# Low half of q in two zero-padded tiles per head pair, in a ten-phase transformer kernel

## The chip, the cores and the metric

The program runs on one core of a Trainium2 chip. The metric is the device time of one execution in microseconds (us), the median of several runs. Times in the profile are counted from the first instruction of the profiled execution. Engines: PE is TensorE (PEld its weight loads), DVE is VectorE, ACT ScalarE, POOL GpSimd, SP SyncE.

## The reference

One sequence of 512 tokens with 1024 features goes through two stacks. The first has two layers of half-step feed-forward, mixer, half-step feed-forward. Its mixers are a hybrid (8 heads of chunkwise retention and 8 heads of dilated attention) and a stick-breaking attention with 16 heads. The second stack has two layers of a mixer and a squared-ReLU feed-forward; its mixer has pooling and 8 heads of a sparse attention (NSA) in two groups, with a branch over compressed keys and two branches over all causal keys. All heads have 64 features. In every attention the scores are products of q and k over these 64 features:

```
s = einsum('...nqd,...nkd->...nqk', qb, kb) * dh ** -0.5      # dilated, NSA
z = einsum('bhqd,bhkd->bhqk', q_blk, kf) * dh ** -0.5         # stick-breaking
scores = einsum('bhnid,bhnjd->bhnij', qc, kc) * decay_in      # retention
```

Inputs, weights and the result are float32.

## The kernel before

**Precision.** Products keep near float32 accuracy by splitting each factor in a high half h (rounded to the type that TensorE multiplies) and a low half l, the rest. A projection's product is h h + h l + l h: three matmuls, lines 326 to 328 (`mm3`), or 734 to 737 where tokens are the output's rows (`tok_k`).

**Phases.** The order is F00, M0, F10, F01, M1, F11, N0, G0, N1, G1. F and G are feed-forwards, M0 the hybrid mixer, M1 the stick-breaking one, N0 and N1 the NSA mixers. The activations stay in SBUF, features on the partitions. Weights come in pieces of 512 KB over SyncE's queue and are split by ScalarE (L297) and by VectorE or, in N, GpSimd (L298).

**Order of the work in a mixer.** The class `Side` puts attention work between the matmuls of the projections. A unit, usually one head, goes through stages: A the scores, B the transposes or sums, C the product with v. A stage is put out once a planned time of products lies behind the stage before it (`N_LAT`, `M1_LAT`, `M0_LAT`); what a stage costs is a fixed number that its function returns. Within an engine the instructions run in the order in which they were put out, which a planner has fixed before.

**Two heads in one tile.** A pair tile has head A's 64 features in rows 0 to 63 and head B's in rows 64 to 127. `stacks` (L742 to 767) makes from it for q: Q with [qhA; qhA] and [qhB; qhB], and QL with [qlA; qlB]; for k: [khA; klA] and [klB; khB]. A score is then two matmuls. The first has all 128 rows and gives qh kh + qh kl at once; the second takes the low half of q with the high half of k of the same head and has the 64 rows of this head:

```
nc.tensor.matmul(ps[:, o:o + N], lhsT=Q[:, hd, qs], rhs=K[:, hd, :N], start=o == 0, stop=False, **kw)     # L861
nc.tensor.matmul(ps[:, o:o + N], lhsT=QL[sl, qs], rhs=K[sl, hd, :N], start=False, stop=True, **kw)        # L862
```

These two lines (`sm_scores`) serve dilated attention and NSA's two branches. For a head the queries go in four tiles of 128, and the causal part gives 512, 384, 128 and 256 columns (`PARTS`), eight matmuls in all. Retention has the same pair at L983 and L985 (`ret_A`), stick-breaking at L1140 and L1142 (`A` of `phase_M1`), there with two halves of the queries: blocks of 128 and 256 columns, then 256, 256, 128 and 256.

**NSA's compressed branch.** `Kc` holds the compressed keys of the two groups in six stationary tiles, the last two for QL (L1398 and L1399). `Vc` holds the compressed values [vh | vl] in rows of 32, so that the product with them (L1456) has 32 rows.

**Around it.** After the scores VectorE takes the row extremum (L866) and ScalarE the exponential (L868); VectorE and ScalarE scale (L877, L879); TensorE transposes (L892); ScalarE and VectorE split the result pTa, pTb (L336, L337); TensorE multiplies by v (L905), and `av_evac` (L908 to 914) adds the two row halves by way of a small tile avt. `n_consts` (L1241) loads the constants of an N phase over GpSimd's queue while the phase before runs: among them the mask cmask and the pooling weights pw. w1, the first layer for the compressed keys and values, is loaded at L1364 within N, and fl (L1498) is its input.

Of the kernel before, what the change touches and what calls it, by code (L numbers as in the profile page):

```python
# [64 lines left out]
# Mixers: PSUM banks (TAGS), the side work's share and latencies (R, LAT, DELAY, CAP; see Side), the ranges of the  # L65
# output projection (OUT), buffers
# [8 lines left out]
M0_AV = 2  # L75
# [18 lines left out]
# tiles of 512, 384, 256 and 128 columns: the part (bank) that holds each, and where  # L94
# [77 lines left out]
class Kern:  # L172
# [34 lines left out]
    # ---------------------------------------------------------------- weights  # L207
# [124 lines left out]
    def split(self, h, l, src, scale=None, leng=None):  # L332
        """h, l with h + l = scale * src; scale None, a power of two, or a column."""
# [8 lines left out]
    def rsqrt(self, out, v, n, tag):  # L342
        """out = v ** -0.5 on [P, n]."""
# [8 lines left out]
        if n <= 2:  # L352
            # a column at a time, with the factors as its scalars
# [51 lines left out]
    def token_sums(self, v, which, c0):  # L405
        """v[:, t] = the sums over the features of the squares, for the token tiles from token c0 on."""
# [20 lines left out]
    def bcast(self, col, tag="b"):  # L427
        """[P, n] token columns -> PSUM [P, n * 128], the same row in every partition."""
# [22 lines left out]
    def e_norm(self, hf, L, which, fn):  # L451
        """xg = x / rms(x) * norm * (1 + scale) + shift for a half of the tokens.

        With fn, x is first normed by final_norm; x itself follows in the next phase.
        A generator: it pauses after the sums and after the row of factors.
        """
# [8 lines left out]
        with self.tc.high_priority():  # L465
# [6 lines left out]
            if fn:  # L472
                # of v = mean(x^2) + eps and v2 = mean((x fnorm)^2): both factors are 1 / sqrt(v2 + eps v)
# [24 lines left out]
    def last_tiles(self, ds, rhs, ks, tag, etag, finish, ws=None):  # L498
        """Output tiles ds; before an explicit norm the last ones go by halves of the tokens."""
# [25 lines left out]
    def e_go(self, tag="b"):  # L525
        """The next step of the norms under way."""
# [12 lines left out]
    # ---------------------------------------------------------------- modulation  # L539
# [29 lines left out]
    # ---------------------------------------------------------------- feed-forward  # L569
# [155 lines left out]
    def tok_k(self, o, w, t, k, kc, width):  # L725
        """Token tile t, contraction tile k, which is kc of the weight piece w."""
# [5 lines left out]
        own = width > 256  # else two token tiles share a bank, which one start clears  # L732
# [6 lines left out]
    def v_evac(self, V, o, t, scale):  # L739
        """V[:, t, head] = [vh | vl] of o [P, heads * 64]."""  # L740
        self.split(V[:, t, :, 0:HD], V[:, t, :, HD:], o.rearrange("p (h e) -> p h e", e=HD), scale=scale)

    def stacks(self, pool, kind, src, scale=None, copies=True):
        """q: QA = [qhA; qhA], QB = [qhB; qhB], QL = [qlA; qlB]; k: KA = [khA; klA], KB = [klB; khB]."""
# [13 lines left out]
        if kind == "q":  # L758
            QL = pool.tile([P, S], F32R, name=self.name("ql"), tag="ql", bufs=self.nst[kind])
            low(QL[A], src, A, T[A, 0, :])  # L760
            low(QL[B], src, B, T[B, 1, :])
# [24 lines left out]
    def out_proj(self, gate, cuts):  # L786
        """x += gate * (o @ w_out), in passes over ranges of the contraction: all but the last run beside side work."""
# [13 lines left out]
        def pieces(n):  # L801
            """Weights of output tile after output tile."""
# [44 lines left out]

    def sm_scores(self, pool, Q, QL, K, sl, table, fac):
        """p = exp(s - max s) * fac / den per q tile; Q holds -q / 8 and table the negated addend to s."""
        nc = self.nc  # L850
        hd = 0 if sl.start == 0 else 1
# [3 lines left out]
        for i, qts in enumerate(PARTS):  # L855
            ps = self.ps.tile([P, S], F32, name=self.name("sc"), tag="b")
            for qt in qts:
# [4 lines left out]
                nc.tensor.matmul(ps[:, o:o + N], lhsT=QL[sl, qs], rhs=K[sl, hd, :N], start=False, stop=True, **kw)  # L862
# [35 lines left out]
    def av(self, ps, hl, V, first=True, last=True):  # L898
        """ps [P, S] += [vh | vl]^T (h + l); V(kt) the stationary [P, 128]."""
# [8 lines left out]
    def av_evac(self, pool, ps, o, hd):  # L908
        """o rows of the head = the two row halves of ps added."""
        nc = self.nc  # L910
        n = ps.shape[-1]
        t = pool.tile([HD, S], F32, name=self.name("avt"), tag="avt", bufs=self.navt)
        nc.scalar.activation(t[:, :n], ps[HD:], AF.Copy)
        nc.vector.tensor_tensor(o[HD * hd:HD * hd + HD], ps[:HD], t[:, :n], ALU.add)

    # ---------------------------------------------------------------- retention + dilated
    def rotary(self, pool, ps, cos, sin):
        """Both heads of a feature-major pair tile: ps * cos + swap(ps) * sin."""
# [11 lines left out]
    def phase_M0(self, ph, pool):  # L930
        nc, I = self.nc, self.I
        self.mixer_start()
        tabs = {}
# [34 lines left out]
        def ret_A(u):  # L968
# [4 lines left out]
            sl = slice(64 * hd, 64 * hd + 64)  # L973
            a = self.score_tiles(pool, F32, 0)
            hl = self.score_tiles(pool, F32R, 1)
            for i, parts in enumerate(PARTS):
                ps = self.ps.tile([P, S], F32, name=self.name("sc"), tag="b")
                w = 0
                for kt in (3 - j for j in parts):
# [5 lines left out]
                    nc.tensor.matmul(ps[:, o:o + N], lhsT=K[sl, hd, ks], rhs=QL[sl, kt * P:],  # L985
# [23 lines left out]
        def dil_A(u):  # L1009
            Q, QL, K, hd, h, V, o = u  # L1010
            u.append(self.sm_scores(pool, Q, QL, K, slice(64 * hd, 64 * hd + 64), lnc, None))
# [94 lines left out]
    # ---------------------------------------------------------------- stick-breaking  # L1106
    def phase_M1(self, ph, pool):
        nc, I = self.nc, self.I
        self.tc.keep_in_program_order(nc.scalar.preload_act_table_set("natural_log_exp_and_others"))
        smask = pool.tile([P, 2, 2 * P], F32, name="smask")  # L1110
        nc.gpsimd.dma_start(out=smask, in_=I["sbmask"])
        mraw = pool.tile([P, 2, P], F32, name="mraw")
# [4 lines left out]
        # blocks (key tile, first column, columns, first query) of a half of the queries  # L1117
        # the blocks on the diagonal are the columns from DG on
# [9 lines left out]

        def zap(zs, c, n):
            return zs[c // 512][:, c % 512:c % 512 + n]  # L1130

        def A(u):
            Q, QL, K, hd, h, V, o, half = u
            sl = slice(64 * hd, 64 * hd + 64)
            zs = [self.ps.tile([P, S], F32, name=self.name("z"), tag="z") for _ in BANKS[half]]
            for kt, c, n, q0 in BL[half]:
# [16 lines left out]
            self.pick(M1_MK[0]).tensor_tensor(e[:, DG[half]], e[:, DG[half]], smask[:, 0, :], ALU.mult)  # L1153
# [769 lines left out]
```

## Time and profile before

| | |
|---|---|
| median of 3 runs | 3391.49 us (3389.45 to 3393.52) |
| span of the profiled execution (the page lists this time of it alone) | 3388.5 us |
| median less that span | 3.0 us |
| busy: TensorE, VectorE, ScalarE, GpSimd | 3312.8, 1903.1, 1383.8, 769.6 us |
| matmuls | 15974 |
| HBM read, mean | 326.77 MB, 97 GB/s |

How to read it: a matmul's busy time includes its way through the array, and the next one starts before it ends, so busy times of TensorE overlap and say little about how fast it goes. The distance from the start of one matmul to the start of the next says it. PEclk is the granted clock of TensorE, 1.00 for 2.4 GHz and 0.50 for 1.2 GHz. Approximate places of the phases: M0 382 to 695, M1 1417 to 1736, N0 2090 to 2385, N1 2740 to 3040; the rest is feed-forwards.

### The profile page before, as it was taken

What the parts mean: (1) busy time and instruction counts of PE and PEld (TensorE: products, weight loads), DVE (VectorE), ACT (ScalarE), POOL (GpSimd) and SP (SyncE); (2) the same over time, 40 slices, a digit from 0 to 9 for tenths busy, and PEclk for the clock granted to TensorE, in tenths of its full rate; (3) what the DMA queues carried; (4) which work ended last, traced back from release to release, by engine and by line L of the source; (5) the groups of instructions that cost most, each with busy time, mean ns of one, the idle gap of its engine ahead of it and who ended that gap; (6) DMA issues with size and microseconds to landing.
All of it is one profiled execution on the core that took longest, in us unless ns stands there. A gap on an engine that the chain in (4) does not pass through costs nothing.

```text
span 3388.5 us, 41553 instructions
## 1 busy us (share of the span) xinstructions
PE 3312.8 (98%) x15974; PEld 2711.8 (80%) x15974; DVE 1903.1 (56%) x3115; ACT 1383.8 (41%) x2274; POOL 769.6 (23%) x712
## 2 busy tenths in 40 slices
PE   9999999999999999999999999889999989999999
PEld 7888888778888888888878888767888877688887
DVE  6633576866337634567853346776533377764332
ACT  4222466632223222477742224565322236633222
POOL 3111222121112110135531102442311143311111
PEclk9999999999999999999999999989999999899999
DMA  7623322165325623311123232201333221013222
GB/s 238 211 87 96 110 80 80 63 200 183 93 91 180 205 94 97 99 58 44 57 82 106 89 101 69 79 25 43 97 95 97 90 81 50 19 44 112 94 93 81
DMA packets 102645, 331.56 MB, mean 98 GB/s; under 512 B 11280, under 2 KB 19568, under 8 KB 102448
## 3 DMA queue, kind: packets, MB, share of 16 engines
q1 hardware_dynamic: 84944, 268.67, 24.9%
q0 software_dynamic: 17504, 60.24, 5.8%
q8 instruction: 126, 2.06, 0.3%
q14 instruction: 71, 0.58, 0.1%
HBM read 326.77 MB, written 2.10 MB: 97 GB/s over the span
## 4 chain that ended last, share of the span: by engine, by line
PE 91%; DVE 6%; ACT 1%; issue 1%; DMA 0%; POOL 0%; SPq 0%; ACTq 0%; DVEq 0%; POOLq 0%
PE po L326 10%; PE po L327 10%; PE po L328 10%; PE pu L327 5%; PE pu L328 5%; PE pu L326 5%; PE pg L327 5%; PE pg L326 5%; PE pg L328 5%; PE p L327 4%; PE p L328 4%; PE p L326 4%; PE pp L328 2%; PE pp L326 2%; PE pp L327 2%; PE av L905 2%
## 5 line engine op out<-in xcount | busy, mean ns | idle before, releaser
L297 ACT ACTIVATE wh<-wr 128x1024 fp32r<-128x1024 f32 (+2 forms) x516 | 535.7, 1039 | 1305.6 <-PE po L327 486.2
L298 DVE TENSOR_TENSOR wl<-wr,wh 128x1024 fp32r<-128x1024 f32 (+2 forms) x466 | 579.4, 1244 | 288.0 <-ACT wh L297 260.6
L327 PE MATMUL po<-hid,wh 128*128 128x512 f32 (+1 forms) x1276 | 489.0, 383 | 0.0
L328 PE MATMUL po<-hid,wl 128*128 128x512 f32 (+1 forms) x1276 | 488.3, 383 | 0.0
L326 PE MATMUL po<-hid,wh 128*128 128x512 f32 (+1 forms) x1276 | 487.6, 382 | 0.0
L337 POOL TENSOR_TENSOR hid<-fs,hid 128x512 fp32r<-128x512 f32 x88 | 143.2, 1627 | 876.0 <-ACT hid L336 875.9
L326 PEld LDWEIGHTS po<-hid,wh 128*128 128x128 f32 x1276 | 240.1, 188 | 49.8
L327 PEld LDWEIGHTS po<-hid,wh 128*128 128x128 f32 x1276 | 240.1, 188 | 48.9
L328 PEld LDWEIGHTS po<-hid,wl 128*128 128x128 f32 x1276 | 240.1, 188 | 48.4 <-DVE wl L298 0.5
L327 PE MATMUL p<-xg,wh 128*128 128x512 f32 (+1 forms) x576 | 215.0, 374 | 2.8 <-DVE xg L496 2.8
L328 PE MATMUL p<-xg,wl 128*128 128x512 f32 (+1 forms) x576 | 214.6, 373 | 0.1
L326 PE MATMUL p<-xg,wh 128*128 128x512 f32 (+1 forms) x576 | 213.4, 374 | 1.1 <-ACT fs L650 1.0
L337 POOL TENSOR_TENSOR hid<-g,hid 128x512 fp32r<-128x512 f32 x64 | 85.5, 1337 | 563.9 <-ACT hid L336 563.9
L591 DVE TENSOR_TENSOR fa<-pg,rB 128x512 f32<-128x512 f32 x88 | 60.3, 690 | 213.1 <-PE pg L328 201.1
L594 DVE TENSOR_TENSOR fs<-fs,pu 128x512 f32<-128x512 f32 x88 | 60.2, 686 | 212.8 <-PE pu L328 212.1
L559 DVE SCALAR_TENSOR_TENSOR wm<-wm,cact 128x1024 f32<-128x1024 f32 x96 | 125.6, 1311 | 89.4 <-DMA wm<-in_w_mod 85.9
L689 DVE SCALAR_TENSOR_TENSOR x<-po,modc,x 128x512 f32<-128x512 f32 (+1 forms) x68 | 48.8, 719 | 210.8 <-PE po L328 210.8
L326 PE MATMUL pu<-xg,wh 128*128 128x512 f32 x416 | 165.9, 399 | 0.0
L328 PE MATMUL pu<-xg,wl 128*128 128x512 f32 x416 | 165.6, 398 | 0.0
L327 PE MATMUL pu<-xg,wh 128*128 128x512 f32 x416 | 165.4, 398 | 0.0
L298 POOL TENSOR_TENSOR wl<-wr,wh 128x1024 fp32r<-128x1024 f32 (+2 forms) x50 | 117.6, 2354 | 208.0 <-ACT wh L297 151.4
L620 DVE TENSOR_TENSOR t<-po,rH 128x512 f32<-128x512 f32 (+1 forms) x100 | 66.8, 668 | 170.3 <-PE po L328 170.3
(406 smaller groups left out, 7745.6 us busy)
## 6 DMA issues: line engine op xcount, KB each, us to landing
wr<-in_ffn_w_in SPq DMA_DIRECT2D x174, 512.0 KB, 3.7
wr<-in_w_ff SPq DMA_DIRECT2D x128, 512.0 KB, 3.8
wm<-in_w_mod POOLq DMA_DIRECT2D x96, 512.0 KB, 4.6
wr<-in_ffn_w_out SPq DMA_DIRECT2D x64, 448.0 KB, 3.3
wr<-in_ffn_w_out SPq DMA_DIRECT2D x32, 512.0 KB, 4.5
wr<-in_hyb_qk SPq DMA_DIRECT2D x16, 512.0 KB, 3.7
wr<-in_sb_qk SPq DMA_DIRECT2D x16, 512.0 KB, 3.6
wr<-in_w_out SPq DMA_DIRECT2D x16, 512.0 KB, 3.6
```

What stands on the lines that cost most here:

```text
L297: nc.scalar.activation(h[:, c], t[:, c], AF.Copy)
L298: e.tensor_tensor(l[:, c], t[:, c], _f(h[:, c]), ALU.subtract)
L326: self.gated(lambda: nc.tensor.matmul(out, lhsT=h[:, s], rhs=xh, start=f, stop=False, skip_group_check=True))
L327: nc.tensor.matmul(out, lhsT=h[:, s], rhs=xl, start=False, stop=False, skip_group_check=True)
L328: nc.tensor.matmul(out, lhsT=l[:, s], rhs=xh, start=False, stop=e, skip_group_check=True)
L337: (leng or nc.vector).tensor_tensor(l, src, _f(h), ALU.subtract)
L559: nc.vector.scalar_tensor_tensor(t, t, 1.0, self.cact, ALU.mult, ALU.mult, accum_out=self.modc[L][:, m:m + 1])
L591: nc.vector.tensor_tensor(a, pg, self.rB, ALU.mult)
L594: nc.vector.tensor_tensor(s, s, pu, ALU.mult)
L620: nc.vector.tensor_tensor(t, po[:, cs], self.rH[:, cs], ALU.mult)
L689: nc.vector.scalar_tensor_tensor(x, po[:, cs], gate[:, d:d + 1], x, ALU.mult, ALU.add)
L905: nc.tensor.matmul(o, lhsT=V(kt), rhs=hl[g][:, j, c:c + (NT - kt) * P], start=first and kt == 0 and j == 0, stop=last and kt == NT - 1 and ...
```

## The change

The low halves of q of a pair go in two tiles of 128 rows: QL[:, 0] has qlA in rows 0 to 63 and zeros below, QL[:, 1] zeros above and qlB in rows 64 to 127. Every matmul with QL so takes all 128 rows of K; the other half of K meets zeros. The QL tiles of a mixer, two in M0 and M1 and three in N, are allocated once at the start and used in turn; GpSimd zeroes the idle halves once (`ql_tiles`). The compressed scores use the same four stationary tiles for QL, now with two matmuls for each QL, so the last two tiles of Kc go. The compressed values lie in four tiles of 128 rows of which 32 are not zero. To make room in SBUF, tags are shared, M0 has one avt buffer instead of two, M1's masks are half as large and read through a broadcast, and cmask and pw are loaded within N, after the first projections, into the places of earlier constants.

The diff's core (comments that were dropped and equal edits at other lines are left out):

```diff
-M0_AV = 2
+M0_AV = 1
...
         if kind == "q":
-            QL = pool.tile([P, S], F32R, name=self.name("ql"), tag="ql", bufs=self.nst[kind])
-            low(QL[A], src, A, T[A, 0, :])
-            low(QL[B], src, B, T[B, 1, :])
+            QL = self.qls[self.nql % len(self.qls)]
+            self.nql += 1
+            low(QL[A, 0, :], src, A, T[A, 0, :])
+            low(QL[B, 1, :], src, B, T[B, 1, :])
...
+    def ql_tiles(self, pool):
+        nc = self.nc
+        self.qls = [pool.tile([P, 2, S], F32R, name=self.name("ql")) for _ in range(self.nst["q"])]
+        for t in self.qls:
+            nc.gpsimd.memset(_f(t[64:128, 0, :]), 0.0)
+            nc.gpsimd.memset(_f(t[0:64, 1, :]), 0.0)
...
-                nc.tensor.matmul(ps[:, o:o + N], lhsT=QL[sl, qs], rhs=K[sl, hd, :N], start=False, stop=True, **kw)
+                nc.tensor.matmul(ps[:, o:o + N], lhsT=QL[:, hd, qs], rhs=K[:, hd, :N], start=False, stop=True, **kw)
...
-                    nc.tensor.matmul(ps[:, o:o + N], lhsT=K[sl, hd, ks], rhs=QL[sl, kt * P:],
+                    nc.tensor.matmul(ps[:, o:o + N], lhsT=K[:, hd, ks], rhs=QL[:, hd, kt * P:],
...
-                nc.tensor.matmul(z, lhsT=K[sl, hd, ks], rhs=QL[sl, q0:q0 + n], start=False, stop=end, **kw)
+                nc.tensor.matmul(z, lhsT=K[:, hd, ks], rhs=QL[:, hd, q0:q0 + n], start=False, stop=end, **kw)
...
-        t = pool.tile([HD, S], F32, name=self.name("avt"), tag="avt", bufs=self.navt)
+        t = pool.tile([HD, n], F32, name=self.name("avt"), tag="avt", bufs=self.navt)
...
-        smask = pool.tile([P, 2, 2 * P], F32, name="smask")
+        smask = pool.tile([P, 2, P], F32, name="smask")
...
+        def masked(engine, t, half, m, op):
+            d = t[:, DG[half]].rearrange("p (a c) -> p a c", c=P)
+            self.pick(engine).tensor_tensor(d, d, smask[:, m:m + 1, :].to_broadcast([P, 2, P]), op)
...
-            self.sq[1] = pool.tile([P, S], F32, name="sqacc1")
+            self.sq[1] = pool.tile([P, S], F32, name="sqacc1", tag="cmask")
...
-        C["cmask"] = load("cmask", [S], I["causal"])
-        C["pw"] = load("pw", [4, P], I["pool_w_2"][L])
...
-        Kc = pool.tile([P, 6, P], F32R, name="Kc")
-        Vc = pool.tile([P, 2, P], F32R, name="Vc")
+        Kc = pool.tile([P, 4, P], F32R, name="Kc")
+        Vc = pool.tile([P, 4, P], F32R, name="Vc")
...
-        for j in range(6):
-            nc.scalar.activation(Kc[:, j, :], cmask[:, 0:P], AF.Copy, scale=0.0)
+        for t in (Kc, Vc):
+            nc.gpsimd.memset(_f(t), 0.0)
...
+        C["pw"] = C["load"]("pw", [4, P], I["pool_w_2"][L])
+        cmask = C["load"]("cmask", [S], I["causal"])
         w1 = []
...
-                        nc.tensor.matmul(ps, lhsT=Kc[:, 2 * i + h, :], rhs=Q[:, h, :], start=i + h == 0, stop=False)
-                    nc.tensor.matmul(ps, lhsT=Kc[:, 4 + i, :], rhs=QL, start=False, stop=i == 1)
+                        k = Kc[:, 2 * i + h, :]
+                        nc.tensor.matmul(ps, lhsT=k, rhs=Q[:, h, :], start=i + h == 0, stop=False)
+                        nc.tensor.matmul(ps, lhsT=k, rhs=QL[:, h, :], start=False, stop=i + h == 2)
...
-                    nc.tensor.matmul(ps, lhsT=Vc[r0:r0 + 32, g, :], rhs=pcs[p][j][r0:r0 + 32, :], start=False,
-                                     stop=j == 1, tile_position=(r0, 0))
+                    nc.tensor.matmul(ps, lhsT=Vc[:, r0 // 32, :], rhs=pcs[p][j], start=False, stop=j == 1)
...
-                nc.scalar.activation(Kc[B_ if g else A_, 4 + j // 2, c], _f(kh[:, cg]), AF.Copy)
...
-            for g in range(2):
-                self.split(Vc[:, g, 0:HD], Vc[:, g, HD:], po[:, g * HD:(g + 1) * HD])
+            for j in range(4):
+                r, c = slice(32 * j, 32 * j + 32), slice(j % 2 * HD, j % 2 * HD + HD)
+                self.split(Vc[r, j, 0:HD], Vc[r, j, HD:], po[r, c])
```

## Rows read from the trace of the kernel before

**Rows 1.** The page's chain that ended last: share of the span by engine.
```profile
PE 91%; DVE 6%; ACT 1%; issue 1%; DMA 0%; POOL 0%; SPq 0%; ACTq 0%; DVEq 0%; POOLq 0%
```

**Rows 2.** Timeline, PE, M0's dilated scores: start, us, engine, line, operation.
```profile
561.41 0.39 PE L327 MATMUL pp<-xg,wh 128*128 128x512 f32 x1
561.64 0.40 PE L861 MATMUL sc<-stk,stq 128*128 128x512 f32 x1
561.97 0.49 PE L862 MATMUL sc<-stk,ql 64*128 64x512 f32 x1
562.39 0.44 PE L861 MATMUL sc<-stk,stq 128*128 128x384 f32 x1
562.76 0.44 PE L862 MATMUL sc<-stk,ql 64*128 64x384 f32 x1
563.14 0.33 PE L861 MATMUL sc<-stk,stq 128*128 128x128 f32 x1
563.39 0.32 PE L862 MATMUL sc<-stk,ql 64*128 64x128 f32 x1
563.65 0.38 PE L861 MATMUL sc<-stk,stq 128*128 128x256 f32 x1
563.96 0.38 PE L862 MATMUL sc<-stk,ql 64*128 64x256 f32 x1
564.27 0.50 PE L861 MATMUL sc<-stk,stq 128*128 128x512 f32 x1
```

**Rows 3.** Timeline, PE, N0: 128-row matmuls of 256 and of 128 columns.
```profile
2244.44 0.28 PE L905 MATMUL av<-pTb,V 128*128 128x256 f32 x1
2244.56 0.27 PE L892 MATMUL tr<-c_ident,pta 128*128 128x128 f32 x1
2244.67 0.27 PE L892 MATMUL tr<-c_ident,ptb 128*128 128x128 f32 x1
```

**Rows 4.** Groups by line, PE: xcount | busy us, mean ns | idle before, us.
```profile
L862 PE MATMUL sc<-stk,ql 64*128 64x512 f32 (+3 forms) x160 | 68.4, 428 | 0.0
L1142 PE MATMUL z<-ql,stk 64*128 64x128 f32 (+1 forms) x96 | 35.4, 369 | 0.0
...
L1456 PE MATMUL av<-pcT,Vc 32*128 32x512 f32 x32 | 13.5, 477 | 0.0
L985 PE MATMUL sc<-ql,stk 64*128 64x512 f32 (+3 forms) x32 | 13.1, 411 | 0.0
```

**Rows 5.** Windows: from:to, length, busy of PE, PEld, DVE, ACT, POOL; PEclk; DMA, GB/s.
```profile
1417.00:1448.00 31.00, 31.00 (x187) 27.43 (x186) 17.41 (x33) 15.08 (x21) 1.50 (x3) 1.00 0.32 107
1452.30:1459.10 6.80, 6.80 (x15) 4.66 (x16) 1.21 (x3) 3.46 (x6) 0.73 (x1) 0.50 0.00 1
431.00:695.00 264.00, 257.55 (x1368) 209.06 (x1367) 193.47 (x357) 158.87 (x293) 54.63 (x43) 0.98 0.24 75
1448.00:1736.00 288.00, 284.54 (x1548) 234.31 (x1548) 223.30 (x325) 208.77 (x347) 132.81 (x112) 0.98 0.16 53
1640.00:1690.00 50.00, 50.00 (x260) 40.39 (x259) 44.07 (x69) 38.33 (x66) 23.74 (x22) 1.00 0.14 46
2165.00:2347.00 182.00, 169.79 (x823) 126.38 (x821) 142.21 (x353) 114.27 (x277) 68.06 (x73) 0.93 0.12 38
2815.00:2997.00 182.00, 172.93 (x824) 128.10 (x823) 139.02 (x353) 113.72 (x276) 59.29 (x65) 0.92 0.12 38
```

**Rows 6.** Waits, PE: waiting line <- what ended it: us in total, times, longest.
```profile
PE pm L1502 <- DVE fl L1498: 17.4, 2, 8.8
PE sc L861 <- DVE pTa L337: 9.8, 4, 4.6
```

**Rows 7.** Line L205, GpSimd: duration ns min/median/max, first and last start.
```profile
L205 POOL CAST stq<-stq x16: 604/610/613, 2170.4 to 2887.9; 64x512 fp32r<-64x512 f32 x16
```

**Rows 8.** Tile w in N0, GpSimd's issues of w1's loads, in ns.
```profile
L1364 POOL DMA_DIRECT2D w<-in_cmp_w x4: 536/537/585, 2131.6 to 2133.2; - x4
```

**Rows 9.** Tile rg in M0, VectorE's product behind the gate's evacuation, in ns.
```profile
L957 DVE TENSOR_TENSOR oret<-oret,rg x8: 411/421/428, 535.2 to 540.1; 128x256 f32<-128x256 f32 x8
```

More of the change, by code (lines that the diff above doesn't have):

```diff
@@ L770, in mixer_start @@
         self.late, self.main_done, self.have = [], False, [False] * ND
+        self.nql = 0
+    def ql_tiles(self, pool):
[4 more added lines that the diff above has]
+            nc.gpsimd.memset(_f(t[0:64, 1, :]), 0.0)
     def put_o(self, i, src, scale=None):
@@ L846, in score_tiles, with sm_scores @@
         return t
-    def sm_scores(self, pool, Q, QL, K, sl, table, fac):
+    def sm_scores(self, pool, Q, QL, K, hd, table, fac):
         nc = self.nc
-        hd = 0 if sl.start == 0 else 1
         den = pool.tile([P, NT], F32, name=self.name("den"), tag="den", bufs=3)
@@ L911, in av_evac @@
         n = ps.shape[-1]
-        t = pool.tile([HD, S], F32, name=self.name("avt"), tag="avt", bufs=self.navt)
-        nc.scalar.activation(t[:, :n], ps[HD:], AF.Copy)
-        nc.vector.tensor_tensor(o[HD * hd:HD * hd + HD], ps[:HD], t[:, :n], ALU.add)
+        t = pool.tile([HD, n], F32, name=self.name("avt"), tag="avt", bufs=self.navt)
+        nc.scalar.activation(t, ps[HD:], AF.Copy)
+        nc.vector.tensor_tensor(o[HD * hd:HD * hd + HD], ps[:HD], t, ALU.add)
     def rotary(self, pool, ps, cos, sin):
@@ L932, in phase_M0 @@
         self.mixer_start()
+        self.ql_tiles(pool)
         tabs = {}
@@ L972, in ret_A @@
                 load_dec(h + 1)
-            sl = slice(64 * hd, 64 * hd + 64)
             a = self.score_tiles(pool, F32, 0)
@@ L1010, in dil_A @@
             Q, QL, K, hd, h, V, o = u
-            u.append(self.sm_scores(pool, Q, QL, K, slice(64 * hd, 64 * hd + 64), lnc, None))
+            u.append(self.sm_scores(pool, Q, QL, K, hd, lnc, None))
             return 1.2
@@ L1109, in phase_M1 @@
         self.tc.keep_in_program_order(nc.scalar.preload_act_table_set("natural_log_exp_and_others"))
-        smask = pool.tile([P, 2, 2 * P], F32, name="smask")
+        smask = pool.tile([P, 2, P], F32, name="smask")
         nc.gpsimd.dma_start(out=smask, in_=I["sbmask"])
-        mraw = pool.tile([P, 2, P], F32, name="mraw")
+        mraw = pool.tile([P, 384], F32, name="mraw", tag="e0")[:, :256].rearrange("p (a c) -> p a c", c=P)
         nc.gpsimd.dma_start(out=mraw, in_=I["sbsum"])
@@ L1116, in phase_M1 @@
         self.mixer_start()
+        self.ql_tiles(pool)
         BL = (((1, 0, 128, 128), (0, 128, 256, 0)),
@@ L1133, in A @@
             Q, QL, K, hd, h, V, o, half = u
-            sl = slice(64 * hd, 64 * hd + 64)
             zs = [self.ps.tile([P, S], F32, name=self.name("z"), tag="z") for _ in BANKS[half]]
@@ L1141, in A @@
                 end = (c + n) in (384, 512, 896)
-                nc.tensor.matmul(z, lhsT=K[sl, hd, ks], rhs=QL[sl, q0:q0 + n], start=False, stop=end, **kw)
+                nc.tensor.matmul(z, lhsT=K[:, hd, ks], rhs=QL[:, hd, q0:q0 + n], start=False, stop=end, **kw)
             W = BANKS[half][-1][0] + BANKS[half][-1][1]
-            e = buf("e", half, [1024 if half else 384])
+            e = buf("e", half, [WD[half]])
             hl = buf("sp", half, [2, WD[half]], F32R)
@@ L1152, in A @@
                 nc.vector.scalar_tensor_tensor(e[:, c:c + n], z[:, :n], 0.0, e[:, c:c + n], ALU.max, ALU.add)
-            self.pick(M1_MK[0]).tensor_tensor(e[:, DG[half]], e[:, DG[half]], smask[:, 0, :], ALU.mult)
+            masked(M1_MK[0], e, half, 0, ALU.mult)
             self.copy(E_SPH, hl[:, 0, :W], e[:, :W])
@@ L1160, in A @@
                 self.pick(M1_F[0]).tensor_tensor(e[:, 256:512], e[:, 256:512], e[:, 640:896], ALU.add)
-                f = e[:, 256:].rearrange("p (a c) -> p a c", c=384)[:, :, :256]
+                f = e[:, 128:].rearrange("p (a c) -> p a c", c=384)[:, :, 128:]
                 fhl = buf("sf", half, [2, 2, 256], F32R)
@@ L1189, in B @@
                 nc.scalar.activation(a[:, c:c + n], z[:, :n], AF.Exp)
-            self.pick(M1_MK[1]).tensor_tensor(a[:, DG[half]], a[:, DG[half]], smask[:, 1, :], ALU.min)
+            masked(M1_MK[1], a, half, 1, ALU.min)
             self.copy(E_AHH, ah[:, 0, :W], a[:, :W])
@@ L1245, in load @@
         def load(name, shape, src, parts=P):
-            t = pool.tile([P] + shape, F32, name=f"{name}{L}")[:parts]
+            t = pool.tile([P] + shape, F32, name=f"{name}{L}", tag=name)[:parts]
             nc.gpsimd.dma_start(out=t, in_=src)
@@ L1251, in n_consts @@
         if L == 0:
-            self.sq[1] = pool.tile([P, S], F32, name="sqacc1")
-        gains = pool.tile([P, 4, HD], F32, name=f"gains{L}")
+            self.sq[1] = pool.tile([P, S], F32, name="sqacc1", tag="cmask")
+        gs = pool.tile([P, 8, HD], F32, name=f"gs{L}", tag="pw")
+        gains, swg = gs[:, 0:4, :], gs[:, 4:8, :]
         nc.gpsimd.dma_start(out=gains[:, 0, :], in_=I["q_norm_2"][L:L + 1].to_broadcast([P, HD]))
@@ L1260, in n_consts @@
         C["pe"] = load("pe", [2, 16], I["cmp_pe_2"][L])
-        C["cmask"] = load("cmask", [S], I["causal"])
         C["bmask"] = load("bmask", [NT, 32], I["cmpmask"][:, 0])
         C["vis"] = load("vis", [NT], I["cmpvis"])
-        C["pw"] = load("pw", [4, P], I["pool_w_2"][L])
         C["psc"] = load("psc", [4], I["pool_scale_2"][L])
         C["icnt"] = load("icnt", [4, 16], I["icnt"])
-        swg = pool.tile([P, 4, HD], F32, name=f"swg{L}")
         nc.gpsimd.tensor_copy(swg[:, :, 0:32], gains[:, :, 32:64])
@@ L1277, in n_consts @@
         nc.gpsimd.tensor_tensor(ccs[:, 1], ccs[:, 1], swg[:, 1, :], ALU.mult)
+        C["load"] = load
         return C
@@ L1291, in phase_N @@
         C = self.ncon
-        cmask, bmask, vis, ccs, w2, pe, gt = (C[n] for n in ("cmask", "bmask", "vis", "ccs", "w2", "pe", "gt"))
+        bmask, vis, ccs, w2, pe, gt = (C[n] for n in ("bmask", "vis", "ccs", "w2", "pe", "gt"))
         self.mixer_start()
+        self.ql_tiles(pool)
         self.sqt = self.xnt = ("s2", NS2)
@@ L1404, in A @@
             Q, QL = Qs[p]
-            u.append(self.sm_scores(pool, Q, QL, Ks[b], slice(64 * g, 64 * g + 64), cmask, g4[:, :, 4 * g + p, 1 + b]))
+            u.append(self.sm_scores(pool, Q, QL, Ks[b], g, cmask, g4[:, :, 4 * g + p, 1 + b]))
             return 1.2
@@ L1512, in do_kc @@
             kc = pool.tile([64, HD], F32, name="kc")
-            t = pool.tile([64, HD], F32, name="kct")
+            t = pool.tile([64, HD], F32, name="kct", tag="midk")
             k2 = pool.tile([64, HD], F32, name="kc2")
@@ L1544, in do_vc @@
             pm = first_layer(1, project(1))
-            midv = pool.tile([HD, 2, 4, 32], F32, name="midv")
+            midv = pool.tile([HD, 2, 4, 32], F32, name="midv", tag="avt", bufs=self.navt)
             for r4 in range(4):
@@ L1887, in _consts @@
     m = np.stack([k < q, np.where(k < q, 3.0e38, 0.0)], 1)
-    c["sbmask"] = np.concatenate([m, m], 2).astype(f32)
+    c["sbmask"] = m.astype(f32)
     c["sbsum"] = np.stack([np.where(k >= q, -1.0, 0.0), -np.ones((P, P))], 1).astype(f32)
```

## The prediction

> **What bounds the kernel now.** I read the chain that ended last first: TensorE holds 91% of the span, VectorE 6% [rows 1]. So time that leaves TensorE leaves the kernel, as long as nothing else takes its place. The second view is TensorE's own order of time in a run of attention scores, and there the start of one matmul to the start of the next is what counts, since matmuls overlap. Two neighbours with 128 rows and 512 columns start 0.23 us apart (561.41 to 561.64). In the scores, matmuls with 128 rows and with 64 rows take turns, and both grow: 0.33 and 0.42 us at 512 columns, 0.37 and 0.38 at 384, 0.25 and 0.26 at 128, 0.31 and 0.31 at 256 [rows 2]. Where 128-row matmuls follow each other, 256 columns take 0.12 us and 128 columns 0.11 [rows 3]. The excess at 256 and at 512 columns is the same 0.19 us, so it doesn't go by columns: it goes by the change of rows. A matmul between two neighbours of another row count pays 0.19 (512 columns: 0.42 against 0.23), one with such a neighbour on one side about half of it (0.33 against 0.23). Third, the busy times by stretch: is PE really the limit where the scores are? In the two hybrid and stick-breaking mixers (431 to 695, 1448 to 1736) PE is busy 98 and 99% of the time, VectorE 73 and 78%; in the score stretches of the two NSA phases (2165 to 2347, 2815 to 2997) PE is busy 93 and 95%, VectorE 78 and 76% [rows 5]. VectorE is thus next in line.
>
> **What it removes.** Every 64-row score matmul becomes one of 128 rows with the same columns, so both of its changes of rows go. By instruction groups there are 32 in retention, 160 in the softmax attentions (each unit of one head has four: 512, 384, 128 and 256 columns; so 8 units of retention, 8 of dilated attention and 32 of NSA), and 96 in stick-breaking [rows 4]. Price of a pair (the 128-row matmul and the 64-row one), as the two distances less two undisturbed ones [rows 2, 3]: 512 columns 0.75 - 0.46 = 0.29; 384 columns 0.75 - 2 x 0.175 = 0.40, where 0.175 is my estimate between 0.12 and 0.23; 128 columns 0.51 - 0.22 = 0.29; 256 columns 0.62 - 0.24 = 0.38. At the end of a run the next 128-row matmul pays half a change more, 0.10. A unit of four pairs so saves 1.46 us.
> - M0: 16 units x 1.46 = 23.4 us.
> - N0 and N1: 32 units x 1.46 = 46.7 us.
> - M1: by head, the first half of the queries has a pair of 128 and one of 256 columns (0.67), the second three of 256 and one of 128 (1.43): 16 heads x 2.10 = 33.6 us.
> - Compressed values: 32 matmuls of 32 rows [rows 4], two in each unit of the second branch (b = 1), 16 units. In a row they cost two changes per pair of matmuls, 4 x 0.10 = 0.4 us; 16 x 0.4 = 6.4 us, more where other work comes between them.
>
> **What it adds on TensorE.** The compressed scores multiply QL's two tiles instead of one: one more 512-column matmul for each pair of heads, 8 in all at 0.23 = 1.8 us. PE in all: 23.4 + 46.7 + 33.6 + 6.4 - 1.8 = 108.3 us less.
>
> **What it adds elsewhere.** GpSimd zeroes the idle halves at each phase's start: 4 memsets of 64x512 in M0, 4 in M1, 6 in each N and two of 128x512 for Kc and Vc. The trace has no such memset; the nearest row is GpSimd's 64x512 cast at 0.61 us [rows 7], so between 0 and 20 x 0.61 + 4 x 1.2 = 17 us in all. I take 0: at M1's start GpSimd is busy 1.5 us of 31 [rows 5], and the first low half of q is written a whole projection later. Without that cover it would be at most 2.4 us in M0 and M1 and 6 in each N. The loads of cmask and pw move into N, on GpSimd's queue, ahead of the four loads of w1: two issues at 0.54 us [rows 8], so w1 and the weight split queued behind are up to 1.1 us later, and 512 KB more are to be moved. What covers it: the first layer of the compressed keys waits up to 8.8 us for VectorE's fl, not for w1 [rows 6]; I take 0, with 2 x 1.1 us and a transfer as the other end. The single avt buffer in M0 makes each of 8 gate evacuations wait for a 0.42 us product on VectorE [rows 9]: at most 3.4 us on ScalarE, beside PE's projections, taken as 0. Kc loses ScalarE copies, Vc's split gets four small parts for two, the masks of M1 are read through a broadcast: the same elements or fewer on engines with room, 0 either way. Sharing of tags in SBUF moves no work.
>
> **What is late next.** A faster PE meets VectorE, whose work is unchanged. The fullest stretch in which PE still was busy throughout is 1640 to 1690, with VectorE at 44.07 of 50 us [rows 5]: 0.881. I let no stretch become fuller than that.
> - M0: 264 - 23.4 = 240.6, VectorE 193.5, 0.80: all of it, 23.4.
> - M1: 288 - 33.6, and the clock's share below, 3.4: 251. VectorE's 223.3 / 0.881 = 253.4 allows 34.6.
> - N0: 182 - 25.6 (23.35 of scores, 3.2 of values, less 0.9) = 156.4. VectorE allows 142.2 / 0.881 = 161.4: 20.6.
> - N1: the same 25.6; VectorE allows 139.0 / 0.881 = 157.8: 24.2.
> Sum 102.8 us.
>
> **The clock.** Right behind M1's first scores, 1452.3 to 1459.1, the granted clock is 0.50, the 1.2 GHz level, though PE was busy all 6.8 us [rows 5]; PE had just run such turns of 128 and 64 rows without an idle moment. I expect the lower clock there to go: half of 6.8, 3.4 us, which VectorE's bound in M1 mostly takes. In the N stretches the mean clock is 0.93 and 0.92, so 182 x (0.07 + 0.08) = 27 us were lost to it [rows 5]; there PE also stood idle 12 and 9 us, so I count none of that as won.
>
> **The time.** The profiled execution spans 3388.5 us; the median of the runs is 3.0 above that span. 3391.5 - 102.8 = 3288.7, rounded to 3288.
>
> **A rule against it.** Today a 128-row matmul never has a same-row neighbour inside a score run, so no row shows a padded low-half matmul at work; the nearest are the projections, which use all rows one after the other and start every 0.23 or 0.12 us, with each a stationary tile of its own [rows 2, 3]. The Trainium skill, page "TensorE: Matmul & The Clock Gate", section "Part 3: Packing small matmuls", says that a weight load overlaps a running matmul only where their row groups differ; by that, padding to all rows would put every load in front of its matmul. The trace disagrees with it by the same 0.23 us.
>
> **Rivals.**
> - *The load stays in front.* The excess of 0.19 us would be the stationary tile's load, which no row count hides in a score run. Then nothing goes and 1.8 us come: 3393, no measurable change. Against it: rows of equal height [rows 3]. Together with the case that some matmul keeps its rows: 0.03.
> - *Waits come back.* Scores finish sooner, but what follows them doesn't: in the N phases PE already waits 9.8 us in all for VectorE's pTa to give a bank back [rows 6], and M1's ScalarE is at 209 of 288 us. If half of the gain in M1 and N returns as waits: 23.4 + (33.6 + 51.3) / 2 = 65.9, 3326. Chance 0.24.
> - *The clock stays high.* All of PE's 108.3 us, 3.4 in M1 and the 27 in N: 138.7, 3253. For it, denser PE work; against it, VectorE would have to be over 0.95 full in N. Chance 0.18.
> - *GpSimd is held at phase starts* (slower). The zeroed tiles are the first of each pool and lie where the phase before had its own; if GpSimd's memsets must wait for those, the loads of tables and masks and the sums of squares queued behind stand too. It decides from 103 / 4 = 26 us on at each of the four starts; held through 31 us, as long as M1 runs before its scores [rows 5], four starts give 3288 + 124 = 3412. Against it: GpSimd's queue there is nearly empty, and the tables' loads need freed space today too. Chance 0.02.
>
> **How the numbers follow.** Forecast 0.53, the rivals 0.24, 0.18, 0.03 and 0.02. The range 3250 to 3330 holds the forecast and the nearer parts of the two big rivals; about half of each of these, some 0.2, is left out, and the additions bounded above (17 us of memsets, a few of loads) fit inside. About 0.2% (7 us) is what a measurement of this kernel can tell from no change. Faster by more: 0.53 + 0.24 + 0.18 = 0.95; within: 0.03; slower: 0.02.
>
> **What would show it.** Right: no 64- or 32-row matmul in the score lines and the compressed values; score matmuls 0.23 us apart at 512 columns and 0.11 to 0.12 at 128 and 256; no lower clock right behind M1's first scores; VectorE near 0.88 in M1 and N. Wrong: distances that stay at 0.3 or 0.4 us; new waits of TensorE in M1 for VectorE's or GpSimd's sp, sf and ah, or in N for pta and pTa, as long as the time saved; GpSimd waiting at a phase's start with the tables behind it.

## The result, and the profile after

The changed kernel takes 3307.6 us (median of 4 runs, 3300.3 to 3309.1) against 3392.5 for the kernel before (4 runs, 3389.5 to 3394.4): ratio 0.974, 95% interval 0.973 to 0.976, 85 us less. The forecast was 3288. The profiled execution of after is its fastest: 3300.3 us, span 3298.5, 9.1 under the median; before's lies 4.0 under the median of its four. In these two executions the span falls by 90.0 us.

The chain that ended last, after:

```profile
PE 75%; DVE 11%; issue 5%; ACT 5%; DMA 3%; POOL 2%; POOLq 0%; SPq 0%; DVEq 0%; ACTq 0%
```

Against [rows 1], TensorE holds 75% of the chain for 91%, VectorE 11 for 6 and ScalarE 5 for 1. These shares don't measure TensorE's waits. Some 230 of the 546 us by which the chain now runs over other engines lie in the first 145 us and in the 120 us behind M0, stretches that take about as long as before; there the chain goes by the loads of w_mod and GpSimd, where before's goes by TensorE. What TensorE waits is told by its idle time below.

The first z scores of M1, on PE's timeline after (start, us, engine, line, operation):

```profile
1433.46 0.39 PE L327 MATMUL pp<-xg,wh 128*128 128x512 f32 x1
1433.69 0.22 PE L1154 MATMUL z<-stq,stk 128*128 128x128 f32 x1
1433.75 0.27 PE L1156 MATMUL z<-ql,stk 128*128 128x128 f32 x1
1433.86 0.34 PE L1154 MATMUL z<-stq,stk 128*128 128x256 f32 x1
1434.03 0.28 PE L1156 MATMUL z<-ql,stk 128*128 128x256 f32 x1
1434.15 0.28 PE L1154 MATMUL z<-stq,stk 128*128 128x256 f32 x1
1434.26 0.28 PE L1156 MATMUL z<-ql,stk 128*128 128x256 f32 x1
```

All have 128 rows. At 256 columns starts are 0.11 to 0.12 us apart, where [rows 2] has 0.31. The 512-column scores start 0.23 apart (2130.42 to 2130.65 in N0).

Where the time went, by stretch of attention work (in M0 retention, then the dilated heads; M1 from its first score to F11; N from the first scores to the last product with v). Columns as in [rows 5], but each stretch now ends where its own work does. Before:

```profile
431.20:511.30 80.10, 80.10 (x481) 65.76 (x480) 59.78 (x95) 46.62 (x80) 18.07 (x19) 1.00 0.27 83
511.30:680.20 168.90, 162.47 (x826) 130.98 (x826) 126.94 (x245) 108.52 (x209) 35.95 (x24) 0.98 0.23 72
1448.50:1722.70 274.20, 270.74 (x1490) 222.94 (x1489) 214.65 (x307) 203.85 (x340) 130.82 (x111) 0.99 0.16 53
2173.90:2347.50 173.60, 161.67 (x754) 118.27 (x753) 133.46 (x344) 105.60 (x259) 61.80 (x69) 0.93 0.10 31
2824.10:2997.10 173.00, 164.24 (x753) 119.50 (x751) 130.07 (x344) 104.84 (x258) 52.31 (x61) 0.92 0.10 31
```

After:

```profile
433.90:502.80 68.90, 68.82 (x482) 63.91 (x480) 58.29 (x95) 46.42 (x80) 18.22 (x19) 1.00 0.30 96
502.80:664.30 161.50, 150.82 (x826) 128.19 (x826) 126.39 (x245) 108.48 (x209) 35.30 (x24) 0.99 0.24 76
1433.70:1680.80 247.10, 236.79 (x1490) 209.36 (x1489) 218.21 (x306) 201.65 (x339) 132.85 (x111) 1.00 0.19 58
2130.40:2284.00 153.60, 133.98 (x750) 113.54 (x749) 132.26 (x345) 102.34 (x259) 61.18 (x68) 0.94 0.11 37
2757.40:2907.10 149.70, 136.06 (x756) 113.71 (x755) 130.38 (x346) 103.15 (x259) 51.19 (x60) 0.94 0.11 36
```

The first two numbers of a row split a stretch: its length, and PE's busy time in it. Their difference is PE's idle time.

| stretch | length, us | PE busy | PE idle | forecast: PE, length |
|---|---|---|---|---|
| M0 retention | -11.2 | -11.3 | +0.1 | -11.7, -11.7 |
| M0 dilated | -7.4 | -11.7 | +4.3 | -11.7, -11.7 |
| M1 | -27.1 | -34.0 | +6.9 | -37.0, -34.6 |
| N0 | -20.0 | -27.7 | +7.7 | -25.6, -20.6 |
| N1 | -23.3 | -28.2 | +4.9 | -25.6, -24.2 |
| sum | -89.0 | -112.8 | +23.7 | -111.6, -102.8 |

The five stretches hold 89.0 of the 90.0 us. TensorE's part is nearly as worked out; 23.7 us of it came back as waits, where 9 were allowed. A part of the 112.8 is the clock and not the rows: length times what PEclk lacks of 1.00, summed over the five rows, is 32.1 us before and 19.8 after. That is an estimate of at most 12.3 us (PE also stood idle in some of it), where the forecast has 3.4.

Two waits that grew or are new (after: waiting line <- what ended it, us in total, times, longest; before has the second once, with 0.4 us, and not the first):

```profile
PE z L1154 <- ACT a L1203: 2.8, 1, 2.8
PE sc L870 <- DVE mn L875: 2.6, 1, 2.6
```

In N0 the list is an old one with larger numbers. Before, then after:

```profile
PE sc L861 <- DVE pTa L337: 7.0, 2, 4.6
PE py L326 <- ACT pwhl L336: 2.2, 1, 2.2
PE tr L892 <- DVE ptb L879: 2.2, 1, 2.2
```

```profile
PE sc L870 <- DVE pTa L337: 7.3, 3, 4.5
PE tr L901 <- DVE ptb L888: 4.7, 2, 2.5
PE py L326 <- ACT pwhl L336: 4.4, 1, 4.4
```

GpSimd's new memsets (groups by line, columns as in [rows 4]):

```profile
L779 POOL MEMSET ql<- 64x512 f32 x10 | 5.2, 521 | 7.5 <-DVE xg L496 5.3 <-DVE t L620 1.9
L780 POOL MEMSET ql<- 64x512 f32 x10 | 5.2, 520 | 0.5
L1322 POOL MEMSET Vc<- 128x512 f32 x2 | 1.0, 520 | 0.0
```

With Kc's two, equal to Vc's, they are 12.5 us of GpSimd, and TensorE doesn't see them: from a mixer's first projection to its first score it takes 48.7 us in M0 and 31.6 in M1, before and after, and 79.0 and 78.5 in N0.

### The profile page after: what moved, and what is told of

Read it like the earlier page. It is cut to its first block, busy times and chain, and to the rows that moved or that the text cites. A ratio compares the mean times of both kernels' runs of the same rounds, so it can differ in the third digit from the quotient of the medians.

```text
span 3298.5 us, 41567 instructions
## 1 busy us (share of the span) xinstructions
PE 3192.8 (97%) x15982; PEld 2677.9 (81%) x15982; DVE 1903.8 (58%) x3119; ACT 1375.6 (42%) x2258; POOL 784.5 (24%) x736
## 3 DMA queue, kind: packets, MB, share of 16 engines
q1 hardware_dynamic: 84944, 268.67, 25.6%
## 4 chain that ended last, share of the span: by engine, by line
PE 75%; DVE 11%; issue 5%; ACT 5%; DMA 3%; POOL 2%; POOLq 0%; SPq 0%; DVEq 0%; ACTq 0%
PE po L328 9%; PE po L327 9%; PE po L326 9%; PE pg L327 4%; PE pg L328 4%; PE pg L326 4%; PE pu L328 4%; PE pu L327 4%; PE pu L326 4%; PE p L327 4%; PE p L328 4%; PE p L326 4%; DMA wm<-in_w_mod 3%; PE av L914 1%; PE pp L327 1%
## 5 line engine op out<-in xcount | busy, mean ns | idle before, releaser
L326 PEld LDWEIGHTS po<-hid,wh 128*128 128x128 f32 x1276 | 239.8, 188 | 48.7
```

The costliest lines, as they stand in the source:

```text
L326: self.gated(lambda: nc.tensor.matmul(out, lhsT=h[:, s], rhs=xh, start=f, stop=False, skip_group_check=True))
```

## The experiments

**The change of rows.** e1 gives all 288 score matmuls their 64 rows back and keeps everything else of the change: the zeroed tiles, memsets, loads, shared tags, Kc and Vc. e2 does so in M1 alone. e3 has the 64 rows of e2, but puts out all 128-row matmuls of a unit before its 64-row ones, so that a head has 4 changes of rows and not 12.

```diff
-                nc.tensor.matmul(z, lhsT=K[:, hd, ks], rhs=QL[:, hd, q0:q0 + n], start=False, stop=end, **kw)
+                sl = slice(64 * hd, 64 * hd + 64)
+                nc.tensor.matmul(z, lhsT=K[sl, hd, ks], rhs=QL[sl, hd, q0:q0 + n], start=False, stop=end, **kw)
```

e3 also has, ahead of the low half's matmul:

```diff
+            for kt, c, n, q0 in BL[half]:
+                z = zap(zs, c, n)
+                ks = slice(kt * P, (kt + 1) * P)
```

> The changed kernel, but every score matmul with the low half of q takes 64 rows of the padded tiles again (288 matmuls). All the rest of the change stays. Theory, the change of rows costs 0.19 us per matmul between neighbours of another height: nearly the whole gain goes, 3388 us (3378 to 3396), and score distances are 0.31 and 0.42 us again. Rival, part of the gain came from the rest (places in SBUF, order of the work, loads moved): the time stays below 3365.

> The changed kernel, with 64 rows for the low half in the stick-breaking mixer M1 alone (96 matmuls). Theory: M1 gets back the 27 us that it lost, 3334 us (3328 to 3340), and the granted clock is 0.50 again right behind M1's first scores, at about 1437 to 1445. Rival, the clock there fell for another reason: it stays 1.00 and the time is 3 us lower.

> As the run with 64 rows in M1, but within a unit all 128-row matmuls come first and then all 64-row ones, so a head has 4 changes of rows instead of 12, with the same 96 matmuls of 64 rows. Theory, the change is what costs: a third of the 27 us comes back, 3316 us (3311 to 3320), and 64-row matmuls behind each other are 0.12 us apart at 256 columns. Rival, a 64-row matmul is slow by itself: 3334 us as without grouping.

Measured: e1 3385.1 us, 0.998 of before (0.997 to 0.999); e2 3329.4, 0.982 (0.980 to 0.984); e3 3320.5, 0.979 (0.977 to 0.980). M1 in the three profiles (windows; for e2 and e3 also the 7 us that follow its first scores), e1:

```profile
1456.60:1730.60 274.00, 270.55 (x1490) 222.87 (x1489) 214.37 (x307) 203.75 (x340) 130.92 (x111) 0.99 0.16 53
```

e2:

```profile
1431.80:1705.80 274.00, 270.52 (x1490) 223.04 (x1489) 214.42 (x307) 203.64 (x340) 130.97 (x111) 0.99 0.16 53
1435.70:1442.50 6.80, 6.80 (x16) 4.69 (x16) 1.47 (x3) 3.30 (x6) 0.73 (x1) 0.50 0.00 0
```

e3:

```profile
1433.20:1691.10 257.90, 253.37 (x1490) 215.77 (x1489) 215.14 (x307) 202.49 (x340) 131.77 (x111) 1.00 0.17 56
1437.00:1444.00 7.00, 7.00 (x44) 6.26 (x44) 4.46 (x7) 5.82 (x9) 1.48 (x2) 1.00 0.00 0
```

With 64 rows M1 is as long as before, 274.0 against 274.2, and the 1.2 GHz level is back right behind its first scores, for the same 6.8 us. So the rows alone make the difference, and what the change adds around them costs nothing here. The order tells the rest: e3 has the same matmuls with the same rows as e2 in another order, and M1 takes 10.8 us more than after's 247.1 where e2 takes 26.9. Of e2's 26.9 the clock has 3.4 (6.8 us at half). With 4 of 12 changes a cost by the change would be 23.5 / 3 = 7.8; a cost by the 64-row matmul would be 23.5 again. The measured 10.8 is 3.0 above the first, which stays open, and far from the second. PE's timeline of e3 shows a group pay once (4 matmuls to a line):

```profile
1433.97 0.73 PE L1154 MATMUL z<-stq,stk 128*128 128x256 f32 x4
1434.63 0.73 PE L1160 MATMUL z<-ql,stk 64*128 64x256 f32 x4
1435.30 0.50 PE L1154 MATMUL z<-stq,stk 128*128 128x128 f32 x2
```

Four matmuls of 64 rows take 0.67 us from start to start (1434.63 to 1435.30), four undisturbed ones of 256 columns 4 x 0.12 = 0.48: 0.19 for the two ends of the group, the price that one matmul between other rows pays in [rows 2].

e1 ends 8 us under before. The compressed branch, which e1 keeps, was to give 4.6 (6.4 less 1.8); that the 8 are its work is not shown. e1's retention, N0 and N1:

```profile
431.20:515.70 84.50, 84.50 (x482) 69.05 (x480) 59.98 (x95) 46.65 (x80) 17.89 (x19) 0.94 0.24 79
2182.40:2351.20 168.80, 156.72 (x750) 117.75 (x749) 130.90 (x345) 104.08 (x259) 59.52 (x68) 0.92 0.10 33
2829.30:2994.10 164.80, 156.84 (x756) 117.42 (x755) 131.51 (x346) 104.13 (x259) 51.07 (x60) 0.95 0.10 33
```

Retention took 84.5 us for before's 80.1; there its mean granted clock was 0.94 for 1.00, which is 5 us. N0 and N1 are 4.8 and 8.2 us shorter than before's though their scores have 64 rows. So of the 20.0 and 23.3 us that after gains there, the rows of the scores give 15.2 and 15.1: PE's busy time falls by 22.7 and 20.8, and 7.5 and 5.7 of that come back as idle time. In N1 the clock (0.95 in e1 for 0.92 in before) is 5.6 us of the rest; what else it is stays open.

**The compressed values.** e4 gives the product with Vc its 32 rows back.

```diff
-                    nc.tensor.matmul(ps, lhsT=Vc[:, r0 // 32, :], rhs=pcs[p][j], start=False, stop=j == 1)
+                    nc.tensor.matmul(ps, lhsT=Vc[r0:r0 + 32, r0 // 32, :], rhs=pcs[p][j][r0:r0 + 32, :], start=False,
+                                     stop=j == 1, tile_position=(r0, 0))
```

> The changed kernel, with 32 rows again in the 32 products with the compressed values. Theory, 0.4 us for two of them and PE sets the time in N: 6 us more, 3313 to 3314 us (3311 to 3316). Rival, N now goes by VectorE: under 2 us more.

Measured: 3310.6 us, 0.976 (0.975 to 0.978). N0 is 2.8 us longer, N1 1.4 (156.4 and 151.1). A second profile of after itself (e12, below) has 154.8 and 150.9, so 4 us at most, and the medians can't tell this part from nothing.

**Is VectorE the limit in N?** The forecast let no stretch be fuller of VectorE than 0.881. `N_SCL` says which engines scale P in turn. e5 moves scalings from VectorE to ScalarE, e6 does the same to the kernel before, e9 moves them all to VectorE.

```diff
-N_SCL = 'VVA'
+N_SCL = 'VA'
```

(e9: `'V'`.)

> The changed kernel, with every second instead of every third scaling of probabilities in N on ScalarE: 11 of 64 scalings in each layer go from VectorE, about 0.62 us each, so 7 us of its 132 to 133 in the score stretch of N (154 and 150 us long). Theory, after the change VectorE sets the time in N (0.86 and 0.87 full, the ceiling that the forecast used is 0.88): each layer's stretch gets 5 to 8 us shorter, 3294 us (3290 to 3300). Rival, the waits in N are of chains and not of a full VectorE: ScalarE's scaling takes as long, so within 3 us of the changed kernel.

> The same edit on the kernel before. Theory, there TensorE set the time in N and VectorE was 0.76 to 0.78 full: within 3 us of before (3389 to 3396). Rival, VectorE already set the time in N before: 10 us less or more, and the change had gained there for another reason.

> The changed kernel, with all 64 scalings in a layer of N on VectorE: 21 more at about 0.62 us, 13 us more of VectorE's time and as much less of ScalarE's. Theory, VectorE being full sets the time of N: 8 to 13 us more in each layer's score stretch, 3325 to 3333 us. Rival, the chain of a unit through both engines sets it, and where a scaling runs matters little to its length: 0 to 4 us more in each layer, 3308 to 3316 us.

Measured: e5 3312.0 us, 0.976 (0.975 to 0.978); e9 3309.3, 0.975 (0.974 to 0.976); neither can be told from after. e6 3382.1, 0.997 of before (0.996 to 0.998). N0 and N1 (windows), of after's second profile:

```profile
2132.20:2287.00 154.80, 135.16 (x751) 114.47 (x750) 132.79 (x345) 102.45 (x259) 61.15 (x68) 0.93 0.11 36
2765.20:2916.10 150.90, 137.23 (x756) 114.86 (x755) 130.45 (x346) 103.10 (x259) 51.18 (x60) 0.93 0.11 36
```

of e9:

```profile
2132.40:2290.00 157.60, 135.86 (x760) 112.93 (x759) 141.72 (x367) 94.32 (x239) 63.51 (x69) 0.95 0.11 36
2765.40:2915.70 150.30, 135.33 (x754) 113.03 (x753) 133.43 (x367) 93.52 (x238) 51.92 (x60) 0.95 0.11 36
```

of e5:

```profile
2130.60:2288.20 157.60, 137.54 (x757) 116.54 (x756) 131.10 (x335) 108.59 (x271) 60.10 (x68) 0.94 0.11 36
2763.80:2917.00 153.20, 135.13 (x754) 114.79 (x753) 129.18 (x335) 108.08 (x270) 50.80 (x60) 0.94 0.11 35
```

The fourth number is VectorE's busy time. In e9 it has 8.9 us more in N0 and 3.0 in N1, and the stretches change by +2.8 and -0.6; VectorE is 0.90 and 0.89 full. In e5 it has 1.7 and 1.3 less, where 7 were meant, and both stretches are 2 to 3 us longer. So N's length doesn't go by VectorE's load, and 0.881 is no ceiling. In e6 N0 gained 2.2 us and N1 7.5; the mean clock of N1 was 0.96 there for before's 0.92, so whether the edit itself helps the kernel before stays open.

**Do the stages come too soon?** TensorE is faster, the planned leads are those of before. A lead is the planned time between a stage and the next, `M1_CAP` how far scores may run ahead of the stage behind them (`Side`). e7 lowers the cap; e8 gives M1's second stage more lead; e10 does so in M0's dilated heads and N too; e11 goes further, with part of it ahead of the third stage.

```diff
e7   -M1_CAP = (4, 2)                +M1_CAP = (3, 2)
e8   -M1_LAT = (0, 12, 3)            +M1_LAT = (0, 14, 3)
e10  -M0_LAT = ((0, 10), (0, 6, 6))  +M0_LAT = ((0, 10), (0, 8, 6))
     -M1_LAT = (0, 12, 3)            +M1_LAT = (0, 14, 3)
     -N_LAT = (0, 8, 6)              +N_LAT = (0, 10, 6)
e11  -M0_LAT = ((0, 10), (0, 6, 6))  +M0_LAT = ((0, 10), (0, 6, 8))
     -M1_LAT = (0, 12, 3)            +M1_LAT = (0, 16, 3)
     -N_LAT = (0, 8, 6)              +N_LAT = (0, 8, 8)
```

> The changed kernel, with the cap in M1 such that a unit's scores need the sums of the unit three before instead of four before, so that they don't wait for a PSUM bank that ScalarE still reads (2.8 us once, at 1607). Theory, M1 fell short of its 33.6 us by new waits for banks: up to 3 us less, 3305 us. Rival, waits for the sums' inputs come from the shorter lead: the cap takes lead away, 0 to 6 us more.

> The changed kernel, with 14 instead of 12 us of planned products between a unit's scores and its sums in M1. Theory, the scores now take less than planned, so the chain of softplus, split and sums comes too late for the products, and M1 has waits of some 6 us for sf, sp and a: 2 to 5 us less, 3303 to 3306 us. Rival, the waits are for PSUM banks, which a longer lead holds for longer: 2 to 6 us more.

> The changed kernel, with 2 us more of planned products between scores and what follows them in dilated attention (8 instead of 6), stick-breaking (14 instead of 12) and N (10 instead of 8); the stages don't touch each other, so each is read by itself. Theory, the shorter scores left too short a lead: M0's dilated part 2 to 4 us less, M1 2 us less, N 2 to 5 us less in each layer, 3296 us in all (3290 to 3301). Rival, the leads are not what is short, and units held longer in PSUM cost as much as they give: 0 to 6 us more.

> The changed kernel, with 2 us more between transposes and the product with v in dilated attention (8 instead of 6) and in N (8 instead of 6), and 4 us more between scores and sums in stick-breaking (16 instead of 12). Theory of the short lead: N 0 to 3 us less in each layer, M1 2 to 4 us less than with 12; 3300 us (3293 to 3305). Rival, as for the other leads: 0 to 6 us more.

Measured: e7 3311.5 us, 0.976 (0.975 to 0.977); e8 3302.3, 0.974 (0.972 to 0.975); e10 3309.0, 0.975 (0.973 to 0.976); e11 3317.2, 0.977 (0.976 to 0.979). M1, up to F11's first matmul, changes by +3.2, -2.2, -2.2 and +6.4 us. Its mean clock was 0.99 in e7 and 0.98 in e11 for after's 1.00, which is 2.5 and 5.1 us of theirs. Two us more of lead in M1 may give 2. M1 in e8:

```profile
1432.00:1676.90 244.90, 236.51 (x1489) 209.64 (x1488) 213.50 (x306) 201.94 (x339) 128.58 (x111) 1.00 0.18 59
```

No other lead helped: M0's dilated part, N0 and N1 are 4.3, 3.2 and 5.0 us longer in e10 than in after, and 5.6, 2.1 and 2.0 in e11. With these leads, the waits that came back don't go away by planning them later.

**The kernel after once more.** e12 is the changed kernel, unedited.

> The changed kernel as it is, once more. It tells how far stretches and clocks of one and the same kernel lie apart between profiles: 3307 us (3303 to 3311), and by both theories stretches within 3 us of the first profile's, apart from stretches with a lower clock.

Measured: 3309.1 us, 0.975 (0.973 to 0.976). Its profiled execution spans 3309.2 us, 10.7 more than the first one. The mean granted clock is 0.983 for 0.987: in lost time, 3309.2 x 0.017 less 3298.5 x 0.013, 13 us. That is enough for the 10.7, so the two executions may differ by nothing but how long they stand at 1.2 GHz. A stretch is repeated within 2 us.

## Why the forecast was right, and where it was not

The sign, the cause and, nearly, the sum on TensorE were right; the measured 3307.6 lies inside the range, 19 us above the forecast. Of these 19, 13 are in the two profiled executions (90.0 us gained for 102.8), and 6 are that after's profiled execution lay 9.1 us under its median where 3.0 was taken over from before. How the 19 split is chance: e12's profiled execution gains 79.3, and its span equals the median of its runs.

- **Price by the change of rows** (0.19 us for a matmul between neighbours of other height, half on one side): shown by e1, e2 and e3. The sum for M1 leaves out the half change at the end of a run, up to 32 x 0.10 = 3.2 us. The Trainium skill, page "TensorEngine Tiling (Array Packing)", section "Key Properties", says that changing the tiling mode drains TensorE. The trace agrees in that a change costs time, 0.19 us on the matmul between two changes and about 0.10 on each neighbour; that it is a drain no run shows.
- **M0 retention, 11.7:** 11.2.
- **M0 dilated, 11.7:** 7.4. The step that failed is "0.80: all of it". A mean fullness of 0.80 says nothing of the few us in which retention's end and the first dilated heads meet. PE's timeline after, there:

```profile
581.96 0.47 PE L870 MATMUL sc<-stk,stq 128*128 128x512 f32 x1 [1.22 <-DVE pTa L337]
...
586.58 0.39 PE L870 MATMUL sc<-stk,stq 128*128 128x256 f32 x1 [2.58 <-DVE mn L875]
```

  The scores of a head wait in mid-unit for VectorE to give a bank back: 3.8 of the 4.3 us by which PE's idle time grew. VectorE isn't the full one here: from 578 to 587 it is busy 7.47 of 9.00 us, ScalarE 8.78. Just before the work that the longer wait is for, a weight split on VectorE itself waits 1.18 us for ScalarE's wh (window, then VectorE's timeline):

```profile
578.00:587.00 9.00, 5.04 (x32) 3.98 (x30) 7.47 (x17) 8.78 (x16) 2.56 (x2) 1.00 0.21 61
584.27 1.56 DVE L298 TENSOR_TENSOR wl<-wr,wh 128x1024 fp32r<-128x1024 f32 x1 [1.18 <-ACT wh L297]
```

- **M1, 34.6:** 27.1. PE's share was right but for 3 us (34.0 for 37.0). The step that failed is the ceiling's window: 1448 to 1736 reaches 13 us into F11, where VectorE has room (8.15 us busy of 13.3). For M1 alone the same rule gives 274.2 - 214.65 / 0.881 = 30.6. For the other 3.5 the rule offers VectorE's busy time, which rose from 214.65 to 218.21 us with one instruction fewer. It isn't that a denser M1 makes the same instructions longer: e8's M1 is denser still, at 244.9 us, and has 213.50. VectorE is 0.883 full in after and 0.872 in e8, so that it sets M1's length is not shown. The new waits of TensorE are 2.8 us for ScalarE's a and 2.3 for sf and sp.
- **N0 and N1, 20.6 and 24.2:** 20.0 and 23.3, right in size, but by luck, and wrong in reason. The scores' rows were to give 23.35 in each; by e1 they give 15, since 7.5 and 5.7 come back as waits. A part of what the measured gains have beyond that is the clock's (below); the rest is open. e9, with VectorE 0.90 and 0.89 full, takes the ceiling away (after has 0.86 and 0.87). What grew are N0's waits for ptb and pwhl, beside the one for pTa that was there before: a unit goes from engine to engine, and TensorE comes to each station sooner. That the unit's own passage limits N is argued from these waits; no run shortened it.
- **Compressed values, 6.4:** at most 4, by e4.
- **Additions at nothing:** shown as a whole by e1, which has them all and is no slower than before, and for the memsets by the unchanged starts of the mixers. Memsets took 0.52 us, not 0.61 or 1.2.
- **The clock:** the stretch at 1.2 GHz behind M1's first scores went, as expected, and e2 brings it back. In N the mean went from 0.93 and 0.92 to 0.94 (0.93 in e12): 26 us of lost time in before, 18 in after, 21 in e12, so 5 to 8 of N's 43.3 us are the clock's at most, where the forecast counted none. Over all executions the mean clock is 0.977 to 0.983 in before, 0.978 to 0.982 in e1 and 0.983 to 0.987 in after; with 0.980 and 0.9845 the lost time is 68 and 51 us. Up to 17 of the 85 us are thus the clock's, and by e1 they come with the rows. The forecast had 3.4.

The rivals. *The load stays in front* falls with the starts 0.23 us apart. *Waits come back* was partly true: 19.5 us of waits against 90 us that TensorE gave up in M1 and N, where half was supposed. *The clock stays high* fell with 0.94 in N, though part of it came, as said above. *GpSimd is held* fell with the starts of the mixers.

## What to carry to other kernels

Read TensorE by the distance between starts, and look at pairs of neighbours: the excess here didn't go by columns but by what changes from one matmul to the next. A product with half of its rows zero was cheaper here than one of half height between full ones; where padding has no room, matmuls of one height put side by side recovered over half of it in M1 (e3). The fullness of another engine in one stretch is no limit until a run has tried it, and at the least it must be taken from exactly the stretch that is forecast. A mean fullness does not price the meeting of two kinds of units. Look at the clock's part in a gain before a cause gets all of it.

## What was not expected

Of two 128-row matmuls in a row, the second was expected 0.11 us behind a first one of 128 columns. It starts 0.06 us behind it (1433.69 to 1433.75), and the third 0.11 behind that; a first matmul of 256 columns behind such a pair takes 0.17 (1433.86 to 1434.03), and in a run of 256 columns 0.12. So a pair of 128 columns takes 0.17 us and not 0.22, and the next pair of 256 columns 0.29 and not 0.24: together nothing is gained or lost, but a price read from one place in a sequence isn't that of another place.

Also not expected was the clock's part in it: turns of 128 and 64 rows without an idle moment were followed by 6.8 us at 1.2 GHz in M1 of before, e1 and e2 alike, and the same products in groups of equal height, or padded, were not. The turns alone don't decide it: before's retention has them too and stands at 1.00, e1's at 0.94.
